# Two scratch banks for the gate projections, one two-bank sum for the head norm, and the modulation sums moved into the recurrences

## The chip, the cores and the metric

The kernel runs on one core of a Trainium2 chip. The metric is the device time of one execution in microseconds (us). Before the change three runs took 4266.86, 4272.58 and 4274.35 us; their median is 4272.58 us. One further execution was profiled, and all rows of the trace below come from it.

The engines are PE (matrix products; its weight loads are listed apart as PEld), DVE, ACT and POOL (element-wise work) and SP, which only issues DMA transfers. Each engine executes its own list of instructions in order and waits at an instruction whose inputs or output buffer are not ready.

## The reference, cut to what matters

A sequence of 1024 positions of width 1024 passes through one block with three mixers and an MLP, and then through two further layers. The change lies in the first block alone. There the modulation vector, the mixers and the gates are

```
mod = silu(c) @ ada_w + ada_b                      # 6 parts of 1024 columns
h = rms_norm(x) * (1 + sc_m) + sh_m
proj = h @ w_in                                    # ..., columns of b and c, 3 x 1024 gate columns
o_a = diff_attention(...)
o_b = rms_norm(scan_fwd(q, k_f, v, la_f) + scan_bwd(q, k_b, v, la_b)) * silu(b_g)
o_c = rms_norm(scan_fwd(q, k, v, la_f) + scan_bwd(q, k, v, la_b)) * silu(c_g)
g_a, g_b, g_c = split(sigmoid(gates))
merged = g_a * (o_a @ w_up_a) + g_b * (o_b @ w_up_b) + g_c * (o_c @ w_up_c)
x = x + gt_m * (merged @ w_out)
```

A scan is the recurrence S_t = diag(a_t) S_(t-1) + k_t v_t, o_t = S_t q_t. Parts 2 to 5 of `mod` (gt_m and the three parts of the MLP) are first used after the mixers.

## The kernel before, in words

All large products are done in three passes, with weights and activations split into a high and a low part (`mm3`, lines 91 to 93): a projection of 128 output columns over half of the positions is 8 x 3 = 24 matmuls of 512 columns.

Partial sums lie in PSUM pools. `mm` has two tiles of two banks each, `tp` two tiles of one bank; `po` and `pj` are one bank each. A tile is given to its next user when its last reader is done.

The order of the instructions on each engine is not written out by hand. A list scheduler orders them by priority with a timeline of its own; program order gives the priority. Work inside `low_priority()` comes after everything else, and so fills what the scheduler takes for gaps. An engine then keeps that order, whatever really happens.

The stage that the change touches follows attention (`branch_a`):

- **Modulation sums** (`ada`, `ada_sums`). For each of parts 2 to 5, eight weight tiles of 512 KB (`wad`, two buffers) are loaded and accumulated by DVE into `aacc` (L337 once, L335 seven times), and eight small products add up the partitions (`pada`, L346). `program` calls all four ahead of `branch_b`.
- **`branch_b`** runs `scan_group` twice (groups 0 and 1, two heads each). A group has a front (gates, decays, running sums), then seven levels of masked products (`pA`, L559: DVE makes differences, L574 to L577, ACT exponentiates, L578 and L579, POOL and DVE multiply by q and k, PE multiplies, DVE writes the masked part, L587), then the loop of states (`ptk`, `pS`, L619), then the outputs (`pO`, L634 and L638), then `head_norm_gate`.
- **`branch_c`** is one such group with four heads and two outputs `pO`, each followed by `head_norm_gate`.
- **Low-priority work**, called `mid`: 24 gate projections (`store_cols`, called with the columns from 3616 on, result to `gD` in DRAM), then `load_T` of the finished rows of `oD` into `oT`, which takes the place of `h` in SBUF, then `merge_ab`, which gates and adds the first two mixers into `mD` (sigmoid L829, products in `po` and `pj`, DVE L833, POOL L835).
- When `branch_c` has stored its rows, `merge_c` reads them (`oC`) and goes on.

`head_norm_gate` before: the square of `pO` is summed over the partitions of a head in two halves, each through `po` (L650), each followed by Ln and Exp on ACT (L498, L499). `store_cols` before: both halves of a projection go through `pj`, and ACT copies each out (L791).

Of the kernel before, what the change touches and what calls it, by code (L numbers as in the profile page):

```python
# [26 lines left out]
class Kern:  # L27
# [614 lines left out]
    def head_norm_gate(self, sp, p, gcol, gate, dst, row):  # L642

        nc = self.nc
        sq = sp.tile([128, 1024], F32, name="xq", tag="xq", bufs=2)
        rs = sp.tile([128, 1024], F32, name="xk", tag="xk", bufs=2)
        nc.scalar.activation(sq, p, AF.Square)
        for h in range(2):
            ps = self.po()
            nc.tensor.matmul(ps, self.bones, sq[:, h * 512:(h + 1) * 512], start=True, stop=True)  # L650
            self.rstd_wide(ps, 64, rs[:, h * 512:(h + 1) * 512])
        nc.vector.scalar_tensor_tensor(sq, p, gcol, rs, op0=ALU.mult, op1=ALU.mult)
        nc.gpsimd.tensor_tensor(sq, sq, gate, op=ALU.mult)
        nc.sync.dma_start(dst[row:row + 128, :], sq)
# [2 lines left out]

        self.nc.sync.dma_start(V, dap(src, 0, [[256, 128], [128 * 256, 8], [1, 256]]))

    def branch_b(self, pD, vD, dst):  # L660

        nc, tc, a = self.nc, self.tc, self.a

# [4 lines left out]
        with tc.tile_pool(name="hb", bufs=1) as sp:  # L668
# [10 lines left out]
            for i in range(2):  # L679
                q = sp.tile([128, 1024], F32, name="hq", tag="hq")  # L680
                sg = sp.tile([128, 1024], F32, name="hg", tag="hg")
                nc.scalar.activation(q, load(q, 0, i), AF.Silu)
                nc.vector.tensor_scalar(q, q, 0.125, None, op0=ALU.mult)
                nc.scalar.activation(sg, load(sg, 3, i), AF.Silu)
                self.exp_ln_table()
                kk, la = [], []
                for d in range(2):
                    k = sp.tile([128, 1024], F32, name="hk%d" % d, tag="hk%d" % d)
                    l = sp.tile([128, 1024], F32, name="hl%d" % d, tag="hl%d" % d)
                    kk.append(k)  # L690
                    la.append(l)
                    z = load(sp.tile([128, 1024], F32, name="hz", tag="xq", bufs=2), 1 + d, i)
                    l2 = self.softplus_neg_abs(z, sp)
                    nc.vector.tensor_scalar(k, z, -1.0, 80.0, op0=ALU.mult, op1=ALU.min)
                    nc.scalar.activation(k, k, AF.Exp)
                    nc.scalar.activation(k, k, AF.Ln, scale=lb[:, 2 * d + i:2 * d + i + 1], bias=self.one)
                    nc.vector.scalar_tensor_tensor(l, z, 0.0, l2, op0=ALU.min, op1=ALU.subtract)
                    nc.gpsimd.tensor_tensor(l, l, k, op=ALU.add)
                    nc.vector.scalar_tensor_tensor(k, z, 0.0, l2, op0=ALU.max, op1=ALU.add)
                    nc.scalar.activation(k, k, AF.Exp, scale=-1.0)  # L700
                    nc.vector.tensor_scalar(k, k, lb[:, 4 + 2 * d + i:5 + 2 * d + i], None, op0=ALU.mult)
                self.cumsums(*la)
                self.scan_group(sp, q, kk[0], kk[1], la[0], la[1], V[:, :, i * 128:(i + 1) * 128], 2, 1.0,
                                lambda j, p: self.head_norm_gate(sp, p, self.col("hgrn_norm_g"), sg, dst,
                                                                 512 + 128 * i))

    def branch_c(self, pD, vD, dst, mid):

# [71 lines left out]
            self.low, tc.cur_priority = tc.cur_priority, p  # L780
        return cm()

    def store_cols(self, hT, dst, c0, sp, W, m=128):

        nc = self.nc
        wl = self.parts(self.whalf(self.wsrc(self.a["w_in"], 0, 8, c0, m), W=W), m, n=8)
        s = sp.tile([128, 1024], F32, name="gst", tag="gst", bufs=2)
        for h in range(2):
            p = self.pj()
            self.proj_T(wl, hT, p[0:m, :], h)  # L790
            nc.scalar.activation(s[0:m, h * 512:(h + 1) * 512], p[0:m, :], AF.Copy)  # L791
        nc.sync.dma_start(dst, s[0:m, :])
# [1096 lines left out]
    def program(self, ctx):  # L1889
        nc, tc, a = self.nc, self.tc, self.a  # L1890
# [18 lines left out]
        def banks(single):  # L1909
# [6 lines left out]
        oD, x1, x2, x3, h4, x5, h6, eD, cD = [self.dtile(n) for n in (  # L1916
            "oD", "x1", "x2", "x3", "h4", "x5", "h6", "eD", "cD")]
# [8 lines left out]
        sf = opn("fl")  # L1926
# [14 lines left out]
            early()  # L1941
        self.branch_a(h, oD, first)
        sp = opn("ad")
        for s in range(2, 6):
            self.ada(s, sp, "wad", 2, self.po)
        self.branch_b(pB, vB, oD)
        cls("ad")
        oT = []

        def mid():  # L1950
            for j in range(24):
                self.store_cols(h, gD[j * 128:(j + 1) * 128, :], 3616 + j * 128, sf, W)
            cls("h1")
            oT.append([opn("ot%d" % i, "right").tile([128, 6, 1024], FR, name="oT%d" % i) for i in range(2)])
            self.load_T(oD, oT[0], range(6))
            self.merge_ab(oT[0], gD, mD, opn("ox", "right"), sf)
# [50 lines left out]
        def between():  # L2007
            for _ in gmlp:
                pass
            cls("eg", "ew")  # L2010
            return opn("eb")
# [237 lines left out]
```

## Time and profile before

| | |
|---|---|
| median of three runs | 4272.58 us |
| profiled execution, whole | 4270.4 us |
| its span, first to last instruction | 4268.6 us |
| mean granted clock of PE | 0.947 |
| PE busy | 3842.8 us (90%) |
| DVE busy | 2430.1 us (57%) |
| ACT busy | 1909.5 us (45%) |
| POOL busy | 1150.4 us (27%) |

"Busy" counts the instruction's own time; idle time of an engine is told with what ended it. The granted clock is a share of PE's full 2.4 GHz, so that 0.5 is 1.2 GHz. The stage of the change goes from about 532 us (end of attention) to 1198 us (first product of `merge_c`).

### The profile page before, as it was taken

How to read it: one execution, taken by the hardware profiler on the slowest of the kernel's cores; microseconds unless marked ns; L12 is line 12 of the kernel's file. 1: busy time of each engine (PE TensorE's matmuls, PEld its weight loads, DVE VectorE, ACT ScalarE, POOL GpSimd, SP SyncE). 2: the span in 40 equal slices, each digit the busy share in tenths (PEclk: the TensorE clock that was granted, in tenths of full speed). 3: DMA queues.
4: the chain of work that ended last, by engine and by line, in shares of the span. 5: the costliest groups of instructions: out<-in, count | busy, mean ns of one | idle time of the engine just before them, and what ended most of it. 6: DMA issues, size and time to landing. Idle time of an engine off the chain costs nothing. (4 is left out here: it accounts for less than half of the span.)

```text
span 4268.6 us, 57274 instructions
## 1 busy us (share of the span) xinstructions
PE 3842.8 (90%) x21765; PEld 3204.3 (75%) x21765; DVE 2430.1 (57%) x4033; ACT 1909.5 (45%) x3185; POOL 1150.4 (27%) x886
## 2 busy tenths in 40 slices
PE   6999978899879999999799987789988999996997
PEld 5887856667668888888699976667678888785765
DVE  6554585755344233323726576577766776646776
ACT  3444433442333212111436564266634887633665
POOL 2000031331344212122622231011124766520111
PEclk8999989889989999999899998899998999997998
DMA  4222253131552111111223332689831001037996
GB/s 169 60 62 56 65 187 109 55 100 45 183 182 89 59 45 50 44 52 57 92 82 97 84 93 87 242 303 369 284 98 31 26 12 36 15 110 264 376 361 245
DMA packets 318999, 531.01 MB, mean 124 GB/s; under 512 B 36918, under 2 KB 214465, under 8 KB 318724
## 3 DMA queue, kind: packets, MB, share of 16 engines
q1 hardware_dynamic: 309076, 492.23, 33.9%
q0 software_dynamic: 9648, 35.13, 3.3%
q8 instruction: 171, 2.80, 0.3%
q14 instruction: 104, 0.85, 0.1%
HBM read 427.00 MB, written 91.88 MB: 122 GB/s over the span
## 5 line engine op out<-in xcount | busy, mean ns | idle before, releaser
L98 ACT ACTIVATE whi<-wraw 128x1024 fp32r<-128x1024 f32 (+2 forms) x497 | 512.7, 1040 | 761.5 <-PE py L93 213.7
L99 DVE TENSOR_TENSOR wlo<-wraw,whi 128x1024 fp32r<-128x1024 f32 (+2 forms) x409 | 501.7, 1243 | 375.6 <-ACT whi L98 363.6
L99 POOL TENSOR_TENSOR wlo<-wraw,whi 128x1024 fp32r<-128x1024 f32 (+2 forms) x88 | 207.3, 2356 | 1152.3 <-ACT whi L98 1089.4
L91 PE MATMUL pj<-h,whi 128*128 128x512 f32 (+1 forms) x592 | 254.0, 429 | 43.4 <-ACT gst L791 41.0
L92 PE MATMUL mm<-h,whi 128*128 128x512 f32 x640 | 255.0, 398 | 2.9 <-POOL h L99 1.8
L91 PE MATMUL mm<-h,whi 128*128 128x512 f32 x640 | 253.5, 398 | 1.8 <-ACT ms L905 1.4
L93 PE MATMUL mm<-h,wlo 128*128 128x512 f32 x640 | 253.7, 397 | 0.8 <-POOL wlo L99 0.8
L92 PE MATMUL pj<-h,whi 128*128 128x512 f32 (+1 forms) x592 | 246.4, 416 | 0.0
L93 PE MATMUL pj<-h,wlo 128*128 128x512 f32 (+1 forms) x592 | 245.5, 415 | 0.2 <-POOL wlo L99 0.2
L927 DVE TENSOR_TENSOR Y<-py,Y 128x1024 f32<-128x1024 f32 x112 | 137.1, 1224 | 133.4 <-PE py L93 133.4
L91 PE MATMUL pgu<-whi,xe 128*128 128x512 f32 x512 | 207.5, 406 | 5.9 <-ACT xe L98 5.9
L91 PE MATMUL py<-whi,mr 128*128 128x512 f32 x512 | 201.7, 394 | 9.4 <-DVE mr L936 8.2
L92 PE MATMUL pgu<-wlo,xe 128*128 128x512 f32 x512 | 205.0, 400 | 0.0
L93 PE MATMUL pgu<-whi,xe 128*128 128x512 f32 x512 | 204.8, 400 | 0.0
L93 PE MATMUL py<-whi,mr 128*128 128x512 f32 x512 | 202.9, 396 | 0.0
L92 PE MATMUL py<-wlo,mr 128*128 128x512 f32 x512 | 202.1, 395 | 0.0
L396 PE MATMUL ptp<-ident,e 128*128 128x128 f32 x1280 | 184.0, 277 | 13.8 <-ACT pf L400 8.3
L1033 DVE TENSOR_REDUCE ast<-ps 128x1 f32<-128x1024 f32 x128 | 156.3, 1221 | 43.7 <-PE ps L93 30.7
L91 PEld LDWEIGHTS pj<-h,whi 128*128 128x128 f32 (+1 forms) x592 | 117.4, 198 | 84.1 <-ACT gst L791 49.9
L396 PEld LDWEIGHTS ptp<-ident,e 128*128 128x128 f32 x1280 | 150.5, 142 | 32.5 <-ACT pf L400 14.8
L402 POOL TENSOR_TENSOR pt<-pf,pt 128x512 fp32r<-128x512 f32 x128 | 164.3, 1284 | 7.9
L99 DVE TENSOR_TENSOR pt<-ptp,pt 128x512 fp32r<-128x512 f32 x192 | 130.0, 686 | 46.4 <-ACT pt L98 45.3
(658 smaller groups left out, 11063.8 us busy)
## 6 DMA issues: line engine op xcount, KB each, us to landing
wraw<-in_moe_w_gate_dram SPq DMA_DIRECT2D x128, 512.0 KB
wraw<-in_moe_w_up_dram SPq DMA_DIRECT2D x128, 512.0 KB
wraw<-in_moe_w_down_dram SPq DMA_DIRECT2D x128, 512.0 KB
wraw<-in_mlp_w_dram SPq DMA_DIRECT2D x64, 512.0 KB
wraw<-in_w_in_dram SPq DMA_DIRECT2D x52, 512.0 KB
wad<-in_ada_w_dram SPq DMA_DIRECT2D x48, 512.0 KB
gD<-gst SPq DMA_DIRECT2D x24, 512.0 KB
wraw<-x SPq DMA_DIRECT2D x20, 512.0 KB
```

Of the source, the lines that this page charges most:

```text
L91: t.matmul(out, l[0], r[0], start=start, stop=False)
L92: t.matmul(out, l[0], r[1], start=False, stop=False)
L93: return t.matmul(out, l[1], r[0], start=False, stop=stop)
L98: nc.scalar.activation(hi, src, AF.Copy)
L99: (nc.gpsimd if leng == "pool" else nc.vector).tensor_tensor(lo, src, hi.bitcast(F32), op=ALU.subtract)
L396: nc.tensor.transpose(p[:, k, :], e[:, (4 * kg + k) * 128:(4 * kg + k + 1) * 128], self.ident)
L402: nc.gpsimd.tensor_tensor(lo, f, hi.bitcast(F32), op=ALU.subtract)
L927: nc.vector.tensor_tensor(y, pv, y, op=ALU.add)
L1033: nc.vector.tensor_reduce(out=st[:, 0:1], in_=pv, axis=AX.X, op=ALU.min)
```

## The change

The third part of the title is two edits: `branch_b` gets a function `between`, which it calls behind each group, and the modulation sums of parts 2 and 3 are made behind group 0, those of parts 4 and 5 behind group 1. Their small products go through the `tp` tiles instead of `po`. `head_norm_gate` sums both halves into one two-bank tile of `mm` (named `pss`), with one Ln and one Exp over 1024 columns. `store_cols` takes a pair of pools for its two halves; the gate projections pass `pj` and `po`, the earlier callers none.

```diff
@@ head_norm_gate
         nc.scalar.activation(sq, p, AF.Square)
+        ps = self.mm("pss")
         for h in range(2):
-            ps = self.po()
-            nc.tensor.matmul(ps, self.bones, sq[:, h * 512:(h + 1) * 512], start=True, stop=True)
-            self.rstd_wide(ps, 64, rs[:, h * 512:(h + 1) * 512])
+            nc.tensor.matmul(ps[:, h, :], self.bones, sq[:, h * 512:(h + 1) * 512], start=True, stop=True)
+        self.rstd_wide(ps.rearrange("p a b -> p (a b)"), 64, rs)
...
@@ branch_b
-    def branch_b(self, pD, vD, dst):
+    def branch_b(self, pD, vD, dst, between):
...
                                 lambda j, p: self.head_norm_gate(sp, p, self.col("hgrn_norm_g"), sg, dst,
                                                                  512 + 128 * i))
+                between(i)
...
@@ store_cols
-    def store_cols(self, hT, dst, c0, sp, W, m=128):
+    def store_cols(self, hT, dst, c0, sp, W, m=128, ps=None):
...
-            p = self.pj()
+            p = ps[h]() if ps else self.pj()
...
@@ program
-        for s in range(2, 6):
-            self.ada(s, sp, "wad", 2, self.po)
-        self.branch_b(pB, vB, oD)
+        ps = lambda name: self.tp(name).rearrange("p a b -> p (a b)")
+
+        def sums(i):
+            for s in (2 + 2 * i, 3 + 2 * i):
+                self.ada(s, sp, "wad", 2, ps)
+        self.branch_b(pB, vB, oD, sums)
...
-                self.store_cols(h, gD[j * 128:(j + 1) * 128, :], 3616 + j * 128, sf, W)
+                self.store_cols(h, gD[j * 128:(j + 1) * 128, :], 3616 + j * 128, sf, W, 128, (self.pj, self.po))
```

The scheduler makes a new order of this on every engine. Places on DVE, PE and ACT show it. (Behind the edits a line of the changed kernel has a number higher by one to five: L791 is L793 there, L829 is L831.)

DVE before, in the masked products of group 0 (`hl`, `hk` decays and keys, `lm` the masks, `A` the masked scores): the modulation sums stand inside the levels.

```order
L574 TENSOR_TENSOR xq<-hl_4576 128x64x8
L575 TENSOR_TENSOR xq<-hl_4592 128x64x8
L576 TENSOR_TENSOR xk<-hl_4576 128x64x8
L577 TENSOR_TENSOR xk<-hl_4592 128x64x8
L335 SCALAR_TENSOR_TENSOR aacc<-wad,cond,aacc 128x1024
L587 COPY_PREDICATED A<-lm_4547,pA 128x2x512
L584 TENSOR_TENSOR xk<-xk,hk_4575 128x64x8
L585 TENSOR_TENSOR xk<-xk,hk_4591 128x64x8
```

DVE now, in the loop of states of group 0 (`st` the states, L619): there the sums of parts 3 and 4 stand, 16 instructions; eight more stand in the loop of group 1, and the eight of part 2 in the front of group 0.

```order
L619 SCALAR_TENSOR_TENSOR st_4788<-st_4788,el,pS 64x64 x2
L347 TENSOR_TENSOR mod<-pada,vc 128x8
L337 TENSOR_SCALAR aacc<-wad,cond 128x1024
L335 SCALAR_TENSOR_TENSOR aacc<-wad,cond,aacc 128x1024
L619 SCALAR_TENSOR_TENSOR st_4742<-st_4742,el,pS 64x64 x2
```

The levels of group 0 have lost their sums, and the loop of states has got them.

PE before, where the gate projections (`h`, through `pj`) end and the products of `merge_ab` (`oT`) begin. Both outputs of `branch_c` stand ahead of this place, its head norms behind the last product of `merge_ab`.

```order
L91 MATMUL pj<-h_97,whi 128x512
L92 MATMUL pj<-h_98,whi 128x512
L93 MATMUL pj<-h_97,wlo 128x512
L91 MATMUL po<-oT_6972,whi 128x512
L91 MATMUL pj<-oT_6972,whi 128x512
L92 MATMUL po<-oT_6976,whi 128x512
L93 MATMUL po<-oT_6972,wlo 128x512
```

PE now, at the same seam: the last gate products go through `po`, and it stands in the middle of the masked products of `branch_c`.

```order
L91 MATMUL po<-h_97,whi 128x512
L92 MATMUL po<-h_98,whi 128x512
L93 MATMUL po<-h_97,wlo 128x512
L559 MATMUL pA<-xq,xk 128x128 x32
L91 MATMUL po<-oT_6966,whi 128x512
L91 MATMUL pj<-oT_6966,whi 128x512
L92 MATMUL po<-oT_6970,whi 128x512
L93 MATMUL po<-oT_6966,wlo 128x512
```

The number of 512-column gate products (of 1152) and of `merge_ab` products (of 288) that PE has passed when it comes to a place is, before and now: first `pA` of group 0: 96 and 84; its first `pS`: 240 and 234; its first `pO`: 336 and 401; first `pA` of group 1: 448 and 576; its first `pS`: 576 and 725; its first `pO`: 667 and 882; first `pA` of `branch_c`: 767 and 1008; its first `pS`: 960 and none of `merge_ab`, now all 1152 and 94 of `merge_ab`; the end of its second output: 1079 and none, now all of both. Between the sums of the head norm of group 0 (`pss`) and the first `pA` of group 1 PE now has 151 gate products.

ACT before, from the last level of masked products of `branch_c` into its loop of states (`kn`, L604): exponentials (L578, L579, L597), the split of gate weights (L98) and the copies of gate results (L791).

```order
L578 ACTIVATE xq<-xq 128x1024
L579 ACTIVATE xk<-xk 128x1024
L98 ACTIVATE whi<-wraw 128x1024
L791 ACTIVATE gst<-pj 128x512 x2
L597 ACTIVATE xk<-xk 128x1024
L604 ACTIVATE kn<-ptk 128x512 x2
```

ACT now, in the same levels: sigmoids of `merge_ab` (L831) and the splits of `oT` stand between the exponentials, with a load of the function table at each change from one to the other.

```order
L578 ACTIVATE xq<-xq 128x1024
L831 ACT_TABLE_LOAD
L831 ACTIVATE whi<-whi 128x1024
L579 ACT_TABLE_LOAD
L579 ACTIVATE xk<-xk 128x1024
L98 ACTIVATE oT_6966<-oT_6970 128x1024 x6
L831 ACT_TABLE_LOAD
L831 ACTIVATE gG<-gG 128x1024
```

From the first sigmoid of `merge_ab` up to the last `kn` of `branch_c` there are now 13 such loads; before there were none in that stretch.

## Rows read from the trace of the kernel before

**Rows 1.** Span and mean granted clock of the core.

```profile
core 0: 4268.6 us, clock 0.947
```

**Rows 2.** Busy time of each engine in stretches of the stage (from:to in us, length, PE, PEld, DVE, ACT, POOL busy with the number of instructions, granted clock of PE, DMA share, GB/s). The cuts are: end of attention, first `pA`, first `pS` and end of the outputs of group 0; first `pA`, first `pS`, end of outputs of group 1; first `pA`, first `pS`, end of outputs of `branch_c`; end of the gate projections; end of `merge_ab`; first product of `merge_c`.

```profile
532.00:595.00 63.00, 50.61 (x261) 42.83 (x262) 50.49 (x65) 29.77 (x36) 29.71 (x13) 0.86 0.61 203
595.00:691.00 96.00, 68.48 (x458) 56.37 (x456) 79.11 (x84) 27.06 (x30) 22.35 (x7) 0.84 0.48 148
691.00:728.00 37.00, 34.83 (x190) 27.32 (x190) 9.91 (x30) 6.95 (x11) 5.48 (x3) 1.00 0.30 91
728.00:773.00 45.00, 32.81 (x119) 24.30 (x120) 21.69 (x34) 36.23 (x39) 19.14 (x9) 0.85 0.23 78
773.00:837.00 64.00, 54.23 (x397) 43.38 (x395) 54.60 (x54) 21.20 (x25) 22.21 (x9) 0.89 0.14 42
837.00:879.00 42.00, 40.22 (x210) 30.51 (x210) 10.39 (x31) 8.80 (x13) 2.38 (x1) 1.00 0.23 71
879.00:908.00 29.00, 26.87 (x91) 18.22 (x89) 13.55 (x30) 15.44 (x17) 12.90 (x8) 0.88 0.51 176
908.00:1010.00 102.00, 93.23 (x714) 74.93 (x713) 78.44 (x76) 37.23 (x43) 32.76 (x12) 0.87 0.19 58
1010.00:1066.00 56.00, 52.49 (x286) 39.73 (x284) 19.38 (x60) 8.87 (x12) 2.37 (x1) 1.00 0.14 48
1066.00:1087.00 21.00, 18.06 (x77) 13.50 (x73) 0.00 (x0) 5.88 (x7) 0.00 (x0) 1.00 0.26 76
1087.00:1169.00 82.00, 71.99 (x290) 56.85 (x290) 32.99 (x37) 26.84 (x29) 31.64 (x14) 0.92 0.59 204
1169.00:1198.00 29.00, 6.21 (x9) 1.41 (x7) 4.82 (x5) 18.54 (x20) 9.47 (x4) 0.61 0.56 189
```

**Rows 3.** What PE waited for between 532 and 1198 us: engine, line, waited for: us in total, times, longest.

```profile
PE pj L91 <- ACT gst L791: 38.8, 19, 6.6
PE mm L91 <- ACT oC L98: 15.1, 1, 15.1
PE pA L559 <- DVE A L587: 11.7, 6, 5.7
PE pada L346 <- DVE aacc L335: 8.3, 1, 8.3
PE po L650 <- ACT xk L498: 8.0, 3, 3.8
PE pA L559 <- DVE xk L585: 7.5, 3, 4.6
PE po L91 <- ACT oT L98: 6.8, 1, 6.8
```

**Rows 4.** PE in order of time around one wait for the copy of a gate result (start us, us, engine, line, operation, idle before it and what ended it).

```profile
748.64 0.40 PE L92 MATMUL pj<-h,whi 128*128 128x512 f32 x1
748.87 0.39 PE L93 MATMUL pj<-h,wlo 128*128 128x512 f32 x1
755.11 0.80 PE L91 MATMUL pj<-h,whi 128*128 128x512 f32 x1 [5.84 <-ACT gst L791]
755.70 0.63 PE L92 MATMUL pj<-h,whi 128*128 128x512 f32 x1
756.13 0.63 PE L93 MATMUL pj<-h,wlo 128*128 128x512 f32 x1
```

**Rows 5.** The instructions on `aacc` (modulation sums) alone in the first two stretches, columns as in rows 2 without ACT and POOL.

```profile
532.00:595.00 63.00, 1.84 (x16) 1.94 (x16) 17.96 (x10) 0.86 0.61 203
595.00:691.00 96.00, 7.26 (x48) 7.35 (x48) 28.24 (x22) 0.84 0.48 148
```

**Rows 6.** DVE in order of time, two sums that follow each other with nothing between.

```profile
602.17 1.28 DVE L335 SCALAR_TENSOR_TENSOR aacc<-wad,cond,aacc 128x1024 f32<-128x1024 f32 x1 [1.50 <-DMA wad<-in_ada_w_dram]
604.94 1.29 DVE L335 SCALAR_TENSOR_TENSOR aacc<-wad,cond,aacc 128x1024 f32<-128x1024 f32 x1 [1.49 <-DMA wad<-in_ada_w_dram]
```

**Rows 7.** ACT between 1066 and 1198 us by line (count, busy us, mean ns, idle before and releasers): the sigmoids of `merge_ab` (in three kinds of buffer), the split of `oT`, and table loads of the head norms.

```profile
L829 ACT ACTIVATE gG<-gG 128x1024 f32<-128x1024 f32 x8 | 8.5, 1060 | 17.1 <-DMA gG<-gD 15.7 <-issue 1.4
...
L98 ACT ACTIVATE oT<-oT 128x1024 fp32r<-128x1024 f32 x6 | 6.3, 1058 | 3.4 <-DMA oT<-oD 3.4
L498 ACT ACT_TABLE_LOAD x4 | 5.1, 1283 | 0.1
...
L829 ACT ACTIVATE whi<-whi 128x1024 f32<-128x1024 f32 x4 | 4.2, 1060 | 7.6 <-DMA whi<-gD 5.7 <-DVE wlo L99 1.9
L829 ACT ACTIVATE wlo<-wlo 128x1024 f32<-128x1024 f32 x4 | 4.2, 1052 | 6.3 <-DMA wlo<-gD 6.3
```

**Rows 8.** ACT in order of time in the head norm of `branch_c`.

```profile
1169.32 1.28 ACT L498 ACT_TABLE_LOAD   x1
1170.61 0.69 ACT L498 ACTIVATE xk<-po,epsc 128x512 f32<-128x512 f32 x1
```

**Rows 9.** PE in order of time at the end of the stage.

```profile
1176.24 2.08 PE L650 MATMUL po<-xq,bones 128*128 128x512 f32 x2 [3.76 <-ACT xk L498]
1181.13 2.07 PE L650 MATMUL po<-xq,bones 128*128 128x512 f32 x2 [2.81 <-ACT xk L498]
1198.29 1.22 PE L91 MATMUL mm<-oC,whi 128*128 128x512 f32 x2 [15.09 <-ACT oC L98]
```

**Rows 10.** The rest of the execution behind the stage, columns as in rows 2.

```profile
1198.00:4268.00 3070.00, 2806.97 (x16019) 2366.43 (x16019) 1764.59 (x3064) 1442.73 (x2523) 903.17 (x778) 0.96 0.40 134
```

## The prediction

> **What bounds the kernel now.** I read the span and clock first [rows 1], then the stage of the change cut at its milestones [rows 2], then what PE waits for in it [rows 3], then single instructions. All of the sum is made against the profiled execution, 4270.4 us whole and 4268.6 us of span; the median of the runs, 4272.6, is 2.2 us above it, so the result of the sum is raised by that.
>
> The reader is to see two things in rows 2. First, the stage takes 666 us, and PE is busy for 550 of them: 116 us are idle, and in six stretches its granted clock is only 0.84 to 0.89. Second, the stage is made of two parts one behind the other: the recurrences (595 to 1066 us), in which PE has gaps that the gate projections are to fill, and then what is left of the low-priority work (1066 to 1169 us: 21 us of gates, 82 us of `merge_ab`) while DVE is busy for 33 of 103 us and the recurrences have nothing to do. So the price of every microsecond that PE loses inside the recurrences is paid at the end: the filler that did not fit comes behind them.
>
> Rows 3 say where it is lost: 38.8 us in 19 waits for the copy of a gate result out of the single bank `pj`. Rows 4 show the largest kind: PE stands 5.84 us, and then works at a spacing of 0.43 us (755.70 to 756.13) where it had 0.23 us before (748.64 to 748.87): that is the level of 1.2 GHz instead of 2.4. A second bank takes these waits away, since the next half has a bank of its own and 24 matmuls at 0.23 us, 5.5 us, to run while ACT gets to the copy.
>
> **The change part by part.** I go through the stretches of rows 2. Where PE is full (clock 1.00, busy 94% or more) I add or take off the 512-column products that the new order has put in or taken out, at 0.23 us each [rows 4]; where a chain on the other engines sets the pace I keep that pace.
>
> *End of attention to the first `pA`, 63 us.* The chain of the front sets it; the order gives it about the same gate products (84 instead of 96) and still the eight sums of part 2. I take 61: its loads now stand ahead of the first weight tiles of the sums on SP.
>
> *Masked products of group 0, 96 us.* The sums occupy DVE for 28.2 us here [rows 5], and DVE is busy for 79 of 96 us. They go. What is left is 68; the same work in group 1, which has no sums, took 64 [rows 2]. I take 66: a gain of 30.
>
> *States and outputs of group 0, 37 us.* PE is full. The order puts in 167 gate products instead of 96: 71 x 0.23 = 16, so 53. The 16 sums that land here need 16 x 1.28 = 20.5 us of DVE beside its 9.9; at the pace of 2.77 us that two sums have when they wait for their weights [rows 6] they need 44 us. Both fit into 53, so filler sets this stretch, and the sums are hidden by it. If that cover were gone they would cost up to 44 + 10 - 37 = 17 us.
>
> *To the first `pA` of group 1, 45 us.* 175 gate products instead of 112: 40 us of pure PE work, where before 45 passed with gate waits in them. I take 47. The head norm lies in here; instead of two Ln and two Exp of 512 columns there is one each of 1024, which saves fixed time on ACT alone; hidden by the gates, I cost it at nothing. `pss` takes one of two `mm` tiles while `pO` holds the other, so no `pA` can start until the Ln has read it; 151 gate products, 35 us, stand in between and cover that.
>
> *Masked products of group 1, 64 us.* DVE is busy for 54.6. Kept at 64; 11 more gate products go into its gaps.
>
> *States and outputs of group 1, 42 us.* 157 instead of 91 products: 15 us more, 57. The eight sums (22 us at 2.77) are hidden.
>
> *To the first `pA` of `branch_c`, 29 us.* 126 instead of 100 products: 6 us, 35.
>
> Up to here the new kernel is at 383 us where the old one is at 376, but it has passed 1008 of 1152 gate products instead of 767. That is the whole point: 241 products, 55 us, done in time that was lost.
>
> *Masked products of `branch_c`, 102 us.* This is the uncertain term, since the gates run out in it and `merge_ab` begins. PE work goes from 193 products to 238, 10 us on 93.2 busy, so 104 with no gaps. On ACT come 13 table loads of 1.29 us (1169.32 to 1170.61) [rows 8], 17 us. From below, the cost is nothing: ACT is busy for only 37 of 102 us, and POOL and DVE have room. From above everything that ACT does and waits for around these sigmoids stands in front of the exponentials: the loads, 17; 16 sigmoids, 17; their waits for DMA and DVE, 17.1 + 7.6 + 6.3 = 31; the splits of `oT` with their wait, 10 [rows 7]: 75 us. I take 16, near the loads themselves, since a wait for DMA does harm only when an exponential is ready behind it. So 118.
>
> *States and outputs of `branch_c`, 56 us.* 194 products (of `merge_ab`) instead of 119: 17 us, 73.
>
> *Rest of the gates and `merge_ab`, 21 + 82 us.* Nothing is left of them: minus 103.
>
> *Tail, 29 us.* Before, four halves of head norms wait for one another on `po`, 8.0 us in rows 3, with a table load at each step [rows 8, 9]; then the stored rows come back, 15.1 us of idle PE. Now there are two sums. But the second `pO` needs an `mm` tile, and both are held until the first Ln has read `pss`: what goes here is waited for there. I take 33.
>
> Sum: 61 + 66 + 53 + 47 + 64 + 57 + 35 + 118 + 73 + 33 = 607 instead of 666, 59 us less: 4270.4 - 59 + 2.2 = 4213.6, forecast 4213 us.
>
> The Trainium skill's page "ScalarE: Activation LUTs" (section "What ACT_TABLE_LOAD costs") speaks against the change: it puts a switch at about 2.66 us, a load of 1283 ns and a drain of 1380 ns. By it the 13 loads would cost 18 us more, and the time would be an estimated 4231 us. The trace agrees with the load (mean 1283 ns [rows 7]) and shows no drain: the activation starts 1.29 us after the load began [rows 8].
>
> The 3070 us behind the stage [rows 10] have no edit, but the scheduler has swapped some instructions there too. No row has a price for that. I bound it at 9 us on either side, 0.3% of the stretch, and take nothing.
>
> **The rivals.**
>
> *The recurrences give way too (more gain).* All gaps are filled. Of the 116 idle microseconds only the return of the stored rows (15.1), the wait for `oT` (6.8) and half of the waits of `pA` (10) remain [rows 3]: 84 us less, 4270.4 - 84 + 2.2 = 4189 us. For it: the copies' waits also hold up the `pA` queued behind them, so the chain itself gets shorter. Against it: in the levels of group 1 DVE is busy for 85% and sets the pace, whatever PE does.
>
> *The filler has moved, and `branch_c` pays it back (no change).* ACT meets the upper end, 75 us instead of 16: 4213 + 59 = 4272 us. For it: in order on ACT a sigmoid that waits for `gD` holds every exponential behind it. Against it: the sigmoids' buffers are loaded ahead, and most of those waits before were in an engine that had nothing else to do.
>
> *Slower.* The same place, with one more step: a buffer of the sigmoids is freed by POOL's addition (L835), and that now queues behind POOL's products for the levels, so the waits for DMA double from 31 to 62 us: 106 instead of 16, 4303 us. It decides from 75 us of extra time in the two stretches of `branch_c`; above that the gain of the earlier ones is gone. Against it: POOL is busy for 33 of 102 us there [rows 2].
>
> *The change does not do what it says:* the second bank could stay unused if PE's order still put both halves behind one copy. The order has them in turn, so I give this nothing beside the case of no change.
>
> **How the numbers follow.** Forecast 65%, with its own range 4190 to 4242 (the term of 16 between 0 and 40, and the 9 us of the rest). More gain 21%, no change 8%, slower 6%. About 0.2%, 8.5 us, is what a measurement of this kernel can tell from no change; faster by more than that are the first two cases and a little of the third, 87%; within it 7%; slower 6%. The range of 8 in 10 takes in the gain of 4189 with half of its own spread and goes up towards the case of no change: 4165 to 4262.
>
> **What would show it right or wrong.** In the profile after: waits of `pj` or `po` for `gst` of a few microseconds in all instead of 38.8; masked products of group 0 near 66 us; the gates done some 55 us into the masked products of `branch_c`; no stretch of `merge_ab` alone behind the outputs; `mm<-oC` starting near 1139 us. Wrong it would be if the masked products of `branch_c` took 160 us or more, with `xq` and `xk` behind sigmoids in ACT's waits, if the loops of states waited for `wad`, or if the time behind the stage moved by more than 9 us.

## The result, and the profile after

The changed kernel takes 4228.0 us (median of 4 runs, 4223.0 to 4232.8) against 4270.8 us before in the same comparison: a ratio of 0.9901, 95% interval 0.9888 to 0.9915, so 43 us or 1.0% faster. The forecast was 4213 us, with its own range of 4190 to 4242. Its profiled execution took 4223.0 us, the lowest of the four. (Medians below leave out one execution of a later kernel that ran at a granted clock of 0.41.)

The span and clock of the kernel after, which answer to [rows 1]:

```profile
core 0: 4221.2 us, clock 0.950
```

The stage of the kernel after, cut at the same milestones as [rows 2], and behind it the rest of the execution, which answers to [rows 10] (from:to, length, PE, PEld, DVE, ACT, POOL busy with the number of instructions, granted clock, DMA share, GB/s). The cuts are: end of attention; first `pA`, first `pS` and end of outputs of group 0; of group 1; of `branch_c`; first product of `merge_c`; end.

```profile
532.00:587.50 55.50, 45.63 (x241) 38.05 (x239) 42.79 (x60) 29.30 (x35) 20.55 (x11) 0.88 0.62 202
587.50:661.80 74.30, 59.59 (x414) 48.58 (x415) 60.43 (x60) 28.76 (x32) 23.02 (x9) 0.91 0.20 57
661.80:716.50 54.70, 54.50 (x297) 44.19 (x295) 28.64 (x47) 9.17 (x13) 5.88 (x4) 1.00 0.63 200
716.50:766.40 49.90, 45.35 (x179) 34.37 (x179) 27.77 (x33) 33.48 (x36) 20.87 (x9) 0.97 0.42 140
766.40:835.40 69.00, 57.35 (x415) 45.80 (x415) 58.32 (x58) 25.14 (x30) 22.20 (x10) 0.95 0.15 46
835.40:887.30 51.90, 51.90 (x287) 42.37 (x285) 22.55 (x42) 7.91 (x12) 4.87 (x2) 1.00 0.45 142
887.30:922.50 35.20, 35.20 (x140) 25.69 (x140) 11.72 (x23) 17.28 (x19) 10.56 (x7) 1.00 0.54 179
922.50:1054.10 131.60, 108.36 (x759) 86.21 (x759) 100.36 (x97) 70.72 (x73) 47.15 (x18) 0.83 0.33 113
1054.10:1124.30 70.20, 70.19 (x363) 54.60 (x361) 35.41 (x85) 20.14 (x22) 23.47 (x11) 1.00 0.34 115
1124.30:1142.00 17.70, 1.98 (x4) 0.68 (x4) 1.28 (x1) 6.80 (x6) 4.50 (x2) 0.67 0.62 213
1142.00:4221.00 3079.00, 2811.60 (x16019) 2372.07 (x16019) 1767.21 (x3064) 1443.13 (x2523) 901.56 (x778) 0.95 0.40 133
```

One boundary in [rows 2] is not where its list has it: before the change the outputs of group 1 end at 872.6 us and not at 879, so that the stretch with its states and outputs takes 35.8 us and the next one 35.7, where the rows have 42 and 29:

```profile
836.80:872.60 35.80, 34.52 (x189) 26.65 (x187) 9.37 (x30) 5.22 (x9) 2.38 (x1) 1.00 0.19 59
```

Three things are to be seen. The stage fell from 666 to 610 us, which is what the sum had (607). Inside it, four stretches are now filled by PE to the last microsecond (54.50 of 54.70, 51.90 of 51.90, 35.20 of 35.20, 70.19 of 70.20, all at clock 1.00), and the two stretches of gates and `merge_ab` alone behind the outputs are gone. But the masked products of `branch_c` grew from 102 to 132 us, at clock 0.83. And the rest, in which nothing was edited, takes 3079 us instead of the 3070 of [rows 10]: nearly 9 us of the stage's 56 are lost there.

What PE waited for in the stage of the kernel after, from 532 to 1142.1 us, which answers to [rows 3]:

```profile
PE pA L559 <- DVE A L587: 17.8, 10, 4.3
PE mm L91 <- ACT oC L98: 14.7, 1, 14.7
PE pj L91 <- ACT gst L793: 12.5, 5, 5.2
PE ptk L603 <- DVE xk L598: 11.2, 2, 6.3
PE po L91 <- ACT gst L793: 7.2, 4, 2.8
```

The waits for the copy of a gate result went from 38.8 us in 19 to 19.7 in 9 (12.5 on `pj`, 7.2 on `po`). The wait of `pA` for DVE's predicated copies went up, from 11.7 to 17.8.

The end of the stage, PE in order of time, which answers to [rows 9]:

```profile
1125.41 1.98 PE L650 MATMUL pss<-xq,bones 128*128 128x512 f32 x4 [1.12 <-ACT xq L647]
1142.06 1.22 PE L91 MATMUL mm<-oC,whi 128*128 128x512 f32 x2 [14.67 <-ACT oC L98]
```

The three waits of the head norm's halves for one another, 8.0 us in [rows 3], are gone; the stored rows still come back over 14.7 us in which PE has nothing to do.

### The profile page after: what moved, and what is told of

Same layout as the page of the kernel before. It is cut to its first block, busy times and chain, and to the rows that moved or that the text cites. A ratio compares the mean times of both kernels' runs of the same rounds, so it can differ in the third digit from the quotient of the medians.

```text
span 4221.2 us, 57239 instructions
## 1 busy us (share of the span) xinstructions
PE 3826.8 (91%) x21765; PEld 3200.6 (76%) x21765; DVE 2446.6 (58%) x4033; ACT 1915.2 (45%) x3181; POOL 1141.5 (27%) x886
## 5 line engine op out<-in xcount | busy, mean ns | idle before, releaser
L98 ACT ACTIVATE whi<-wraw 128x1024 fp32r<-128x1024 f32 (+2 forms) x497 | 512.8, 1040 | 738.4 <-PE py L93 213.7
L91 PE MATMUL pj<-h,whi 128*128 128x512 f32 (+1 forms) x400 | 163.6, 409 | 15.5 <-ACT gst L793 14.8
L93 PE MATMUL pj<-h,wlo 128*128 128x512 f32 (+1 forms) x400 | 163.0, 407 | 2.9 <-POOL wlo L99 2.6
L92 PE MATMUL pj<-h,whi 128*128 128x512 f32 (+1 forms) x400 | 162.7, 407 | 0.0
L92 PEld LDWEIGHTS mm<-h,whi 128*128 128x128 f32 x640 | 120.5, 188 | 32.2 <-POOL h L99 2.2
```

The costliest lines, as they stand in the source:

```text
L91: t.matmul(out, l[0], r[0], start=start, stop=False)
L92: t.matmul(out, l[0], r[1], start=False, stop=False)
L93: return t.matmul(out, l[1], r[0], start=False, stop=stop)
L98: nc.scalar.activation(hi, src, AF.Copy)
```

## The experiments

The theory, A, was formed from these traces and from the order of each variant: a bank is handed out in the order in which the program asks for it. Whoever asks for `po` earlier in the program has to be done with it first, at whatever priority the later ones run. Then the three edits need one another, because before the change the modulation sums and the head norms of `branch_b` ask for `po` ahead of the gates, and the head norms of `branch_c` ask for it behind the gates and `merge_ab`. The rival B was that the edits add up: 35 us for the second bank, 15 to 28 for the sums, under 10 for the head norm.

### One edit alone

The second bank alone:

```diff
-            p = self.pj()
+            p = ps[h]() if ps else self.pj()
...
-                self.store_cols(h, gD[j * 128:(j + 1) * 128, :], 3616 + j * 128, sf, W)
+                self.store_cols(h, gD[j * 128:(j + 1) * 128, :], 3616 + j * 128, sf, W, 128, (self.pj, self.po))
```

> The kernel before with the second bank for the gate projections alone; modulation sums and head norms stay on `po`. Theory A (the three edits need one another: as long as the sums and the head norms also take `po`, the scheduler puts the gates' second halves behind them, and the gates leave the recurrences): the order has no gate product between the first `pA` of group 0 and the outputs of group 1 (571 before) and 514 instead of 73 behind the outputs of branch_c, 441 x 0.23 = 101 us more there, against some 25 us that the emptier stretches save: about 4347 us, slower by 50 to 100 us. Rival B (the edits add up; the waits for the copy out of one bank, 38.8 us, are the loss): about 4235 us.

Measured: 4360.0 us, ratio 1.0217 (1.0193 to 1.0241): 88 us slower, near theory A's 4347. Rival B falls. The instructions of this kernel on `po` (count, shortest, median, longest ns, first and last start) show why:

```profile
L91 PE MATMUL po<-h,whi x192: 388/397/586, 840.9 to 1172.0; 128*128 128x512 f32 x192
L650 PE MATMUL po<-xq,bones x16: 590/879/1222, 707.4 to 1266.3; 128*128 128x512 f32 x16
```

PE in order of time where the first gate on `po` begins:

```profile
838.98 1.13 PE L650 MATMUL po<-xq,bones 128*128 128x512 f32 x2 [0.78 <-ACT xk L498]
840.89 0.50 PE L91 MATMUL po<-h,whi 128*128 128x512 f32 x1 [0.78 <-ACT xk L498]
```

The first gate half on `po` starts at 840.9, straight after the second half of group 1's head norm. In the kernel after it starts at 556.6. From 577 to 841 us no gate runs at all, since a tile's first half in `pj` is followed by its second half in `po`. In the five stretches from the first `pA` of group 0 to the outputs of group 1 the granted clock is 0.50 to 0.59, little above the lower level; two of them, the masked products of group 0 and of group 1:

```profile
590.70:673.60 82.90, 40.58 (x297) 36.91 (x297) 75.86 (x77) 18.95 (x18) 21.31 (x7) 0.56 0.42 136
756.40:808.10 51.70, 29.47 (x265) 27.45 (x265) 47.11 (x52) 15.43 (x16) 16.77 (x7) 0.59 0.00 1
```

The stage takes 750 us, 230 of them behind the outputs of `branch_c`. What PE waits for in it changes its name:

```profile
PE pA L559 <- POOL xk L563: 56.1, 2, 44.1
PE pA L559 <- DVE xk L585: 35.2, 9, 5.0
PE pj L91 <- ACT gst L791: 6.3, 2, 4.6
```

Of the 38.8 us of waits for the copies in [rows 3] only 6.3 are left, as was meant, and the time went up.

The sums behind each group alone:

```diff
-        for s in range(2, 6):
-            self.ada(s, sp, "wad", 2, self.po)
-        self.branch_b(pB, vB, oD)
+        ps = lambda name: self.tp(name).rearrange("p a b -> p (a b)")
+
+        def sums(i):
+            for s in (2 + 2 * i, 3 + 2 * i):
+                self.ada(s, sp, "wad", 2, ps)
+        self.branch_b(pB, vB, oD, sums)
```

> The kernel before with the modulation sums behind each group alone (on a `tp` bank). Theory A: group 0's masks fall from 96 to about 72 us, states of group 0 and 1 grow to about 45 and 49, the tail has 24 gate products instead of 73, and the waits for the copy out of the one bank stay near 39 us: about 4256 us (gain 15). Rival B (edits add up, and group 0's masks give their 28 us of sums in full): about 4243 us.

Measured: 4284.2 us, 1.0027 (1.0015 to 1.0038): slower, where both had a gain. Masked products, and states and outputs, of group 0 in this kernel, then states and outputs of group 1:

```profile
586.40:653.80 67.40, 54.70 (x385) 44.31 (x385) 58.74 (x58) 25.75 (x28) 23.94 (x9) 0.87 0.18 55
653.80:711.80 58.00, 48.91 (x250) 38.67 (x248) 32.74 (x49) 8.37 (x13) 3.46 (x3) 0.91 0.59 191
...
827.60:880.30 52.70, 45.90 (x250) 36.78 (x248) 23.53 (x42) 7.67 (x12) 2.34 (x1) 0.97 0.38 120
```

The masked products give 28.7 us (96.1 to 67.4), as the row of the sums [rows 5] promised; the two stretches that take the sums grow by 20.5 and 16.9, with only 121 gate products in each (37.5 and 35.8 us before). The kernel after passes 168 gate products in the same states and outputs of group 0, in 54.7 us; here 121 take 58.0. So there filler covers the sums, and here it does not. The stage is 668 us; the rest of what this kernel loses lies behind it (3088 us in its profile, 3070 before).

The head norm alone:

```diff
+        ps = self.mm("pss")
         for h in range(2):
-            ps = self.po()
-            nc.tensor.matmul(ps, self.bones, sq[:, h * 512:(h + 1) * 512], start=True, stop=True)
-            self.rstd_wide(ps, 64, rs[:, h * 512:(h + 1) * 512])
+            nc.tensor.matmul(ps[:, h, :], self.bones, sq[:, h * 512:(h + 1) * 512], start=True, stop=True)
+        self.rstd_wide(ps.rearrange("p a b -> p (a b)"), 64, rs)
```

> The kernel before with the head norm on one `pss` pair alone. Theory A: the recurrences keep their lengths within 3 us each; the tail loses the 8.0 us of waits between the halves and some table loads, 20 gate products and 24 products of merge_ab move ahead: about 4262 us (gain 8 to 10). Rival C (the second `pO` now waits for `pss`): no gain, 4270 us.

Measured: 4248.2 us, 0.9954 (0.9937 to 0.9970): a gain of 23 us, more than twice the expected. PE in order of time, the last head norm in this kernel:

```profile
1075.43 0.44 PE L638 MATMUL pO<-A,gv 128*64 128x128 f32 x4
...
1081.52 1.88 PE L650 MATMUL pss<-xq,bones 128*128 128x512 f32 x4
```

It follows its `pO` after 6 us. Before, the outputs ended at 1066 and the last head norm stood at 1181 [rows 9]: `merge_ab` asked for `po` ahead of it and held it until 1166.8. Now the rows of `oC` come back while `merge_ab` still runs, and the stretch from the outputs to `merge_c` is 83.9 us instead of 132. The recurrences did not all keep their lengths within 3 us, which theory A expected: the states and outputs of `branch_c` take 71.5 us instead of 55.8, with 49 gate products more. The stage is 38 us shorter; behind it the profile has 3087 us, 17 more than before. (The edit also halves the number of Ln and Exp; no run has that part alone.)

### One edit undone

> The kernel after without the second bank: sums behind the groups and head norm on `pss`. Theory A: gates are passed as in the run with the sums alone, waits for the copy near 39 us, tail with 52 gate products and 264 of merge_ab: about 4245 us, so the second bank is worth some 17 us on top of the other two. Rival B (edits add up): 4228 + 35 = 4263 us.

Without the second bank (its diff above, reversed): 4252.1 us, 0.9957 (0.9941 to 0.9974), stage 640 us: 7 above theory A, 11 below rival B. The second bank, which alone costs 88 us, is worth 24 on top of the other two.

> The kernel after with the modulation sums back ahead of group 0 and on `po`. Theory A (edits need one another): no gate product in group 0's masks, where the sums hold `po` (150 after), but 133 to 188 in each stretch from the states of group 0 on; 250 products of merge_ab are left behind the outputs: about 4262 us, 34 above the kernel after. Rival B (edits add up): the sums' move alone is worth 15 to 28, so 4243 to 4256 us.

With the sums back ahead of group 0 on `po` (the diff of the sums, reversed): 4249.0 us, 0.9949 (0.9932 to 0.9966), stage 636 us. The first gate on `po` starts at 683.0, behind the sums; the masked products of group 0 run without any gate. The order is A's, but the time is not: A had put the price at 34 us, it is 21 to 25, and 4249.0 lies inside B's range. By its time this run does not decide between the two.

> The kernel after with the head norm back on `po`, half by half. Theory A: no gate product from the first `pA` of group 0 to the outputs of group 1, 537 behind the outputs of branch_c: about 4322 us, slower than before by 30 to 80. Rival B (edits add up): the head norm is worth under 10 us, 4236 us.

With the head norm back on `po` (its diff, reversed): 4370.8 us, 1.0226 (1.0207 to 1.0244), 98 us slower than before and more than theory A's 30 to 80; rival B (4236) falls again. The first gate on `po` starts at 837.6, again behind the head norm of group 1, and the stage is 753 us. The smallest of the three edits decides whether the change is a gain of 43 or a loss of 98.

The stages of the eight combinations, each from one profile, in us (a second profile of before had 655, one of after 610):

| | neither other | sums | bank | sums and bank |
|---|---|---|---|---|
| head norm on `po` | 666 | 668 | 750 | 753 |
| head norm on `pss` | 628 | 640 | 636 | 610 |

Without the head norm neither of the other edits gains. On top of it, neither alone gains either: by whole time the lower row is 0.9954, 0.9957, 0.9949 and 0.9901 of the kernel before (0.9888 in a second comparison), so only both together do. The 8 to 12 us by which the stages of the single ones are longer are about what the two profiles of before differ by (11).

### Where the masked products of `branch_c` go

```diff
-                nc.scalar.activation(G, G, AF.Sigmoid)
+                nc.scalar.activation(G, G, AF.Copy)
```

> The kernel after with the sigmoids of merge_ab replaced by copies: their part of the computation is left out, so that ACT loads no table between the exponentials of branch_c. Theory F (the masked products of branch_c took 132 instead of 118 us because the sigmoids and their table loads stand in front of the exponentials): the stretch falls to about 108 us, time about 4205 us. Rival G (the stretch is long because PE works at the lower clock and DVE sets the pace; the loads are hidden): 125 to 132 us, 4222 to 4228 us.

Measured: 4218.6 us against 4223.7 for the kernel after in the same comparison. The masked products of `branch_c`:

```profile
921.50:1042.90 121.40, 103.71 (x760) 82.83 (x760) 100.76 (x95) 54.91 (x60) 47.30 (x18) 0.86 0.33 117
```

Between the two expectations: 13 of the 16 table loads of the stretch are gone (70.72 to 54.91 on ACT), and the stretch gives back 10 us, not 24. It still takes 121 us, of which PE is busy for 104, and what holds the other 17 was not shown. Two things can. One is DVE, which is as busy as with the loads (100.76 and 100.36) where before it had 78. DVE by line in this stretch of the kernel after (count, busy us, mean ns, idle before):

```profile
L538 DVE TENSOR_TENSOR_SCAN gl<-onec,gl 128x128 f32<-128x128 f32 x8 | 6.9, 934 | 7.3 <-POOL gl L737 7.3
L99 DVE TENSOR_TENSOR oT<-oT,oT 128x1024 fp32r<-128x1024 f32 x3 | 5.4, 1786 | 1.2 <-ACT oT L98 1.2
L540 DVE TENSOR_TENSOR_SCAN gl<-onec,gl 128x128 f32<-128x128 f32 x8 | 4.8, 671 | 0.0
L835 DVE TENSOR_TENSOR gG<-pj,gG 128x512 f32<-128x512 f32 x4 | 2.7, 681 | 0.0
L835 DVE TENSOR_TENSOR gG<-po,gG 128x512 f32<-128x512 f32 x4 | 2.7, 680 | 0.0
```

Both directions of the running sums (11.7 us, behind 7.3 of waiting for POOL) now lie behind the first `pA`; before, 4.7 of them did. To them come the splits of `oT`, 5.4, and the products with the gates, 5.4.

The other is ACT's order. In the run with copies, ACT still waits 14.4 us in this stretch for gates to come back from `gD` (9.1 on `gG`, the row below, 4.2 and 1.1 on `whi` and `wlo`) and 3.3 for `oD`, and these waits stand among the exponentials. The longest has the exponential of L597 behind it:

```profile
L831 ACT ACTIVATE gG<-gG 128x1024 f32<-128x1024 f32 x6 | 6.2, 1050 | 9.1 <-DMA gG<-gD 9.1
...
1028.92 1.06 ACT L831 ACTIVATE gG<-gG 128x1024 f32<-128x1024 f32 x1 [8.11 <-DMA gG<-gD]
...
1031.69 1.04 ACT L597 ACTIVATE xk<-xk 128x1024 f32<-128x1024 f32 x1
```

The other way to take `merge_ab` out of the levels is to queue what it issues on ACT behind the last exponential of the levels:

```diff
+        if late:
+            late(exps[1])
...
-            self.load_T(oD, oT[0], range(6))
-            self.merge_ab(oT[0], gD, mD, opn("ox", "right"), sf)
-        self.branch_c(pC, vC, oD, mid)
+
+        def late(ins):
+            with self.low_priority(), tc.issue_after(ins):
+                self.load_T(oD, oT[0], range(6))
+                self.merge_ab(oT[0], gD, mD, opn("ox", "right"), sf)
+        self.branch_c(pC, vC, oD, mid, late)
```

> The kernel after, with what merge_ab issues on ACT queued behind the last exponential of branch_c's levels. The order then has 114 gate products and 24 of merge_ab in the masked products (144 and 94 after), 168 in the states and outputs (170) and 96 behind them (24). Theory F2 (merge_ab inside the levels costs more there than its products are worth, whatever the tables): masked products 131 to about 104 us, states and outputs 70, tail 17.8 to about 32, because 96 products, 22 us, lie beside the head norm and the return of the stored rows: 12 to 15 us less, about 4212 us. Rival (the work is only moved, the tail pays back): masked products 115, tail 34, 4226 us, within 0.1% of the kernel after.

> The kernel with merge_ab queued behind the last exponential of the levels, a second time, for a profile at the usual clock; the expectations are those of the first run: masked products of branch_c about 104 us, states and outputs 70, tail about 32 where the expected gain holds (whole time 4212); 115 and 34 where the work is only moved (4226). Its first run measured 4212.6 to 4221.2 us, between the two.

Measured: 4216.5 and 4218.8 us, 0.9872 (0.9856 to 0.9888) and 0.9873 (0.9856 to 0.9890) of the kernel before. Over 8 runs of each, the median is 4217.9 here and 4225.4 for the kernel after, 7.5 us apart; the intervals of the single comparisons touch or overlap. From the second run's profile, the masked products, states and outputs, and tail of `branch_c`:

```profile
923.80:1038.50 114.70, 93.06 (x659) 76.13 (x659) 95.09 (x89) 54.89 (x59) 41.15 (x15) 0.70 0.27 98
1038.50:1111.50 73.00, 72.98 (x374) 56.57 (x373) 37.07 (x84) 21.17 (x22) 23.47 (x10) 1.00 0.41 139
1111.50:1134.00 22.50, 15.94 (x64) 11.88 (x64) 6.37 (x9) 8.73 (x9) 9.95 (x5) 0.95 0.39 134
```

The tail is better than the theory had it (22.5, with 15.9 of work beside the returning rows), the masked products worse (114.7 instead of 104, the rival's 115): with 100 products fewer to fill the gaps the granted clock is 0.70 where it was 0.83. PE is busy for 15.3 us less, where 100 products at 0.23 us are 23, so what it has left to do takes longer. Some half of the expected gain is kept, and it is the fastest version here that computes the whole.

### The 9 us behind the stage

> The kernel after, unchanged. Theory D (the 9 us behind the stage are clock dips that come in one execution and not in another): from the first product of merge_c to the end it takes another number of us than 3079 by 2 to 8, with the difference in the even attention of layer 2 (about 2240 to 2550 us) where the granted clock is under 1.00; median 4228 within 4. Rival E (the swapped instructions in that attention cost 8 us each time): 3079 within 1.5 us, and the same shift of 7 us there.

> The kernel before, unchanged, for a second profile. Behind the stage (from the first product of merge_c to the end) its first profile has 3070 us, and the nine profiles of changed kernels have 3078 to 3092. Theory D (the clock dips fall differently in each execution, and the first profile was a lucky one there): 3075 to 3085 now, with the stage at 666 within 2. Theory H (the order of before in the even attention, which all changed kernels have lost, is worth 8 us each time): 3070 within 2.

> The kernel after with all four modulation sums behind group 1. Behind the stage its order is that of the kernel before but for one instruction on ACT and four matmuls late in the program, while every other changed kernel has lost before's order in the even attention. The stage's order is near that of the kernel after (70 gate products and 127 of merge_ab in the masked products of branch_c, 161 in the states, none behind): stage 606 to 614 us. Theory H (before's order in the even attention is worth 8 us): 3070 within 2 us behind the stage, about 4215 us. Theory D (clock dips fall as they fall in each execution): 3076 to 3085 behind the stage, about 4224 us.

The last is the kernel after with

```diff
-            for s in (2 + 2 * i, 3 + 2 * i):
+            for s in ((), (2, 3, 4, 5))[i]:
```

The rest of the execution in the second profile of before, in that of the sums behind group 1, and in the second profile of after:

```profile
1187.30:4257.30 3070.00, 2806.31 (x16019) 2366.01 (x16019) 1762.72 (x3064) 1443.66 (x2522) 899.80 (x778) 0.96 0.40 134
```

```profile
1153.80:4223.10 3069.30, 2804.48 (x16019) 2364.27 (x16019) 1769.53 (x3064) 1442.82 (x2522) 904.50 (x778) 0.96 0.40 134
```

```profile
1141.80:4222.50 3080.70, 2811.37 (x16019) 2370.16 (x16019) 1766.83 (x3064) 1443.11 (x2522) 904.91 (x778) 0.96 0.40 133
```

The count is as theory H has it. The three executions with the order of before in the even attention have 3069.3 to 3070.3 us behind the stage; the ten with another order have 3077.7 to 3091.6. (The sums behind group 1 gain nothing by it as a whole: 4228.2 us, 0.9898, 0.9881 to 0.9914. Their stage takes 622 us, more than the 606 to 614 expected.) The kernel after, run again, takes 4223.7 us (median of four). Its second profile has 3080.6 us behind the stage, only 1.6 from the first: near rival E's bound, and short of the 2 to 8 of theory D.

But neither the size nor the place is as H and E have it. The kernel with copies in place of sigmoids has, behind the stage, the order of the kernel after on every engine (its data differ), and takes 9 us more there than the first execution of the kernel after:

```profile
1130.90:4219.10 3088.20, 2820.13 (x16019) 2378.98 (x16019) 1764.55 (x3064) 1443.78 (x2522) 907.21 (x778) 0.95 0.40 133
```

In this attention the order of the kernel after leaves that of before only from about 2497 us on, where some rows on PE, ACT and DVE and, at 2513, a transfer of `K` on SP change places with their neighbours. (Ahead of it, some rows of `merge_c` and three on DVE have changed places too.) Counted matmul by matmul from the first product of `merge_c`, its first execution is behind the first profile of before by 0.8 us at 2243, by 6.4 at 2492, where every instruction of this attention stands as before, and by 8.4 at 2565. About the same 20 us of scores in the first and in the second execution of the kernel after:

```profile
2413.50:2433.50 20.00, 17.59 (x98) 15.50 (x99) 16.14 (x41) 13.67 (x39) 3.07 (x2) 0.76 0.32 88
```

```profile
2413.00:2433.00 20.00, 16.72 (x124) 14.69 (x124) 19.48 (x55) 16.67 (x49) 3.07 (x2) 1.00 0.35 92
```

In the first, PE gets 98 matmuls done at clock 0.76; in the second 124 at 1.00. By the same count the second execution is behind by 1.5 us at 2243, by nothing at 2485 and by 2.8 at 2562, and loses another 7.5 after this attention. So time at the lower clock is part of the loss, and where it falls differs between executions of one kernel: that much of theory D is shown. What the three executions near 3070 share, if not chance (they are the lowest three of thirteen), stays open; instructions that are swapped from 2497 us on cannot have cost what was lost in this attention ahead of them.

## Why the prediction was right, and where it was not

The time of 4228 lies 15 us above the forecast and inside its own range. Of these 15 us, 3 are the stage (610 for 607), 9 the rest of the execution, and 3 the place of the profiled execution among the runs: the sum was raised by 2.2 for it, and after the change the median is 5.0 above. By its own terms, in us, predicted and measured:

| stretch | before | predicted | measured |
|---|---|---|---|
| to the first `pA` | 63 | 61 | 55.5 |
| masked products, group 0 | 96 | 66 | 74.3 |
| states and outputs, group 0 | 37 | 53 | 54.7 |
| to the first `pA` of group 1 | 45 | 47 | 49.9 |
| masked products, group 1 | 64 | 64 | 69.0 |
| states and outputs, group 1 | 42 (35.8) | 57 | 51.9 |
| to the first `pA` of `branch_c` | 29 (35.7) | 35 | 35.2 |
| masked products, `branch_c` | 102 | 118 | 131.6 |
| states and outputs, `branch_c` | 56 | 73 | 70.2 |
| rest of gates and `merge_ab` | 103 | 0 | 0 |
| tail | 29 | 33 | 17.7 |
| rest of the execution | 3070 | 3070 | 3079 |

(In brackets, the lengths before by the true end of group 1's outputs. From these the step would have had 51 and 42 where it has 57 and 35.)

*In part luck.* That the stage came out within 3 us is not the merit of the single terms. Three are too short by 13.6, 8.3 and 5.0 us and three too long by 15.3, 5.5 and 5.1, and these cancel.

*Right.* The filler moved into the recurrences and nothing of it is left behind the outputs. The sums are hidden where PE is full: 54.7 measured against 53, at clock 1.00. Where the order gave so many products, 0.23 us each was good to a few microseconds; `mm<-oC` started at 1142 where 1139 had been said.

*Mis-sized: the masked products of `branch_c`.* The step was "104 with no gaps" and "I take 16, near the loads themselves", which make 120; the 118 it took are the old 102 and the 16. The loads are worth 10 (the copies in place of sigmoids). Without them the stretch would still be 121. The step left out that DVE gets 22 us more to do, of which the scans, the splits of `oT` and the gate products are the rows above, and it set ACT's waits for `gD` and `oD` at nothing, of which 17.7 us stand among the exponentials in the run with copies. Which of the two holds the 17 us over 104 stays open. The upper end of 75 and both rivals built on it fell.

The Trainium skill's page "ScalarE: Activation LUTs" (section "What ACT_TABLE_LOAD costs") led to an estimate of 4231 us, nearer to 4228 than the forecast is. That is no point for its drain: by its 2.66 us each, 13 loads would cost an estimated 34.6 us, and taking them away gave 10 in the stretch. In the stretch of the kernel after, too, the activation starts 1.29 us after the load began, and the load starts 0.02 us after the activation before it ended:

```profile
1007.64 1.06 ACT L578 ACTIVATE xq<-xq 128x1024 f32<-128x1024 f32 x1
1008.72 1.28 ACT L831 ACT_TABLE_LOAD   x1
1010.01 1.06 ACT L831 ACTIVATE gG<-gG 128x1024 f32<-128x1024 f32 x1
1011.09 1.28 ACT L579 ACT_TABLE_LOAD   x1
1012.38 1.06 ACT L579 ACTIVATE xk<-xk 128x1024 f32<-128x1024 f32 x1
```

*Mis-sized: the masked products of the two groups*, by 8 and 5. "A few microseconds in all" of waits for copies became 19.7, of which 2.6 and 3.7 lie here; in group 0 PE also waits 6.3 us for `xk` (L598) at the end of the levels. The queued merge, with nearly the same gate products here (148 and 147, against 150 and 149), has no wait for a copy in these two stretches and 1.5 us for `xk`, and took 65.9 and 63.7: so 66 and 64 can be met. The step's "11 more gate products" in group 1 are 21 by the counts of the order (149 for 128); since the queued merge passes nearly as many in 63.7 us, that slip did not cost the 5.

*Mis-sized: the tail*, 33 against 17.7. The step took the old chain over and let the second `pO` wait for `pss`. The profile shows no such wait, because products of `merge_ab` lie between; the first head norm's sums are done at 1115, ahead of the second `pO`, and only the last head norm is left in the tail.

*Wrong: what the head norm's edit does.* "I cost it at nothing" stood at group 1, with only the 8.0 us of waits at the tail. Alone it gains 23 us, and without it the change loses 98. The sum came out because it went along the finished order, in which all three edits act; the attribution of the gain to the bank ("A second bank takes these waits away") did not. [rows 9] had the evidence: a head norm at 1176 for outputs that ended at 1066. It was read as a short chain at the end instead of as a request held up for some 100 us.

*At the edge: "No row has a price for that. I bound it at 9 us on either side".* The rest measured +8.8 in the profiled execution. The prediction was right that the order there had changed and that no row could price it; taking the middle cost 9 us of the 15 by which the forecast is off. One part of the 56 us is before's own spread, too: its second execution took 4259.0 us, with the stage at 655 instead of 666.

*The rivals.* More gain (4189) did not come: the waits for copies, 39 of its 84 idle microseconds, were halved, not removed. Payback in `branch_c` was there in kind, but at some 30 us (the 16 taken and 13.6 more) of the 75 it needed.

## What to carry to other kernels

Before a shared buffer gets a second user, list everyone who asks for it in program order: low-priority filler that asks in between waits for all that stand ahead of it, and holds up all that stand behind it, whatever their priority. Judge edits to one resource in their combinations, since one that was costed at nothing can be what lets the others work. When filler is moved into a chain, add up every engine that the filler uses, not only the one that was idle.

## What the runs showed that was not expected

The granted clock is part of the price of an empty slot. With `merge_ab` queued behind the levels, ACT and DVE had less to do in the masked products of `branch_c`, but the granted clock fell to 0.70 there from 0.83, and 114.7 us came out where 104 had been worked out; with the second bank alone, groups 0 and 1 ran at 0.50 to 0.59, little above the lower level (1.2 GHz). And a stretch of one kernel can run at 0.76 in one execution and at 1.00 in the next, with the same instructions in the same order.
